# Two matmul groups and one split of the next expert, moved into both arms of a data-dependent branch

## Chip, cores and metric

The kernel runs on one NeuronCore of a Trainium2 chip. The metric is the device time of one execution in microseconds (us), as the median of several runs.

## What is computed

One layer of a hybrid decoder on 2048 tokens of width 1024: a normalisation and a combined projection, a gated MLP branch and a gated linear recurrence, their merge, then a mixture of experts (MoE), and last a gated per-layer embedding and a final normalisation. The change touches the mixture of experts alone:

```python
def expert_block(args):                     # for each block of tokens of expert e
    xb, e = args
    return (jax.nn.silu(xb @ w1[e]) * (xb @ w3[e])) @ w2[e]
...
grp_prob = jax.nn.softmax(grp_logits, axis=-1)      # top-1 group of 4
top_l, top_e = lax.top_k(sel_logits, TOP_K)         # top-2 of the 8 experts in it
```

There are 32 experts (N_EXPERTS), with w1 and w3 of 1024 x 512 and w2 of 512 x 1024 each, and 4096 assignments of tokens to experts. How many tokens an expert gets depends on the data: 128 on the average, more for some and fewer for others.

## The kernel before

All products are in float32 precision. The large ones are made of float32r matmuls with each operand split into a high and a low part (hi and lo): ScalarE (ACT) copies the raw chunk into float32r, VectorE (DVE) subtracts the copy from the raw chunk, and TensorE (PE) adds three products, hi x hi, lo x hi and hi x lo.

The experts run one after the other in a loop of 33 turns (lines 1071 to 1110), under a manual schedule: each engine takes its instructions in the order in which the program emits them. Turn i has three experts in hand: `was` (the one before), `now` and `then` (the next). An expert takes its first 128 tokens through the split products. Its w1 and w3 come as eight chunks of 128 rows, its w2 as four. The order within a turn is written out by hand in the string `PART`, a word for each step:

- `h2`, `l2` are the high and low split of chunk 2 (methods `hi`, line 890, on ACT; `lo`, line 896, on DVE), and `H0 L0 H1 L1` those of the next expert's chunks 0 and 1. `v0 u0 v1 u1` split chunks of w2. The split tiles `ehi` and `elo` have five buffers each (`SPL`).
- `P0` to `P7` are the matmul groups of the chunks, six matmuls of 512 columns each (line 905), added up in two PSUM banks `ph` of the pool `ps_a`, which has four.
- `S` is the silu on ACT (line 910) and the product with the other half on DVE (line 911), into the tile `g`. `T` is four PE transposes of `g` (line 916), `G` the split of the result, `B0` to `B3` the matmuls with w2 (line 937), `Y` the copy out and the scattered write. These are steps of `was`, a turn after its P7.
- `X`, `x`, `y` turn and split the next expert's token rows.
- `n` and `m` write branch hints, for POOL and SP and for PE, ACT and DVE.

At the end of the turn stands a branch on the count of `now`, read from a register: with more than 128 tokens all engines run `some(0)` (line 945), for 32 more tokens; inside it stand two more branches, for more than 160 tokens `some(1)`, and for more than 192 `rest`. `some` is a chain: 64 small matmuls `pa` (line 950), a silu on ACT (line 954), a product on DVE (line 955), one transpose on PE (line 956), a copy on DVE (line 958), 32 small matmuls `pz` (line 961), a copy on ACT (line 965) and a scattered write.

```python
with tc.If((code & bit) != 0, preferred_fallthrough_block=True, label=f"more{i}"):
    skip(f"most{i}", code, 2 * bit, BUSY[:1])
    now.some(0)
    with tc.If((code & 2 * bit) != 0, preferred_fallthrough_block=True, label=f"most{i}"):
        ...
```

`skip` writes the hint for a later branch: here that of the inner branch `most`, for PE, ahead of `some(0)`. An engine that passes an arm by must still bring its semaphores to the count that the arm would have brought them to; it does so by event instructions, which stand in the profile on the line of the branch (L1103 for the outer branch, L1106 for `most`, L1109 for `beyond`). A program that skips `some` altogether goes from P7 of `now` over the branch to the first words of the next turn, `S P0 P1 h2 l2 h3 l3 T G P2`, in which S and T belong to the expert just finished and P0, P1, h2 and P2 to the next one.

The weights of the next expert are loaded by SP at the head of a turn (lines 720 and 727), into buffers that the expert before last has read to the end, its branch included.

Of the kernel before, what the change touches and what calls it, by code (L numbers as in the profile page):

```python
# [9 lines left out]
F32R = mybir.dt.float32r  # L10
# [7 lines left out]
BUSY = [mybir.EngineType.PE, mybir.EngineType.Activation, mybir.EngineType.DVE]  # L18
QUEUED = [mybir.EngineType.Pool, mybir.EngineType.SP]
# [5 lines left out]
T = 2048  # L25
D = 1024
KT = D // 128
# [9 lines left out]
EPG = 8  # L37
# [7 lines left out]
SPL = 5  # L45
W2B = 8
HGRN = "forget0 R query0 R decay0 og0 R og20 forget1 R att0 query1 state0 decay1 og1 read0 R og21 forget2 R R R norm0 att1 query2 decay2 og2 state1 forget3 read1 R norm1 att2 og22 og3 query3 R state2 decay3 R G og23 att3 G read2 G state3 norm2 G read3 norm3"
PART = "n S P0 P1 h2 l2 h3 l3 T G P2 B0 X h4 l4 B1 h5 l5 x B2 h6 l6 y B3 h7 l7 P3 P4 Y v0 u0 m P5 v1 u1 P6 H0 L0 P7 H1 L1"
ORDER = [EPG * g + i for i in range(EPG) for g in (0, 1, 3, 2)]
EARLY = 4  # L50
E0 = 0, 0, 2, 2
# [25 lines left out]
def tile_hybrid_block(ctx: ExitStack, tc: tile.TileContext, a, out):  # L77
# [3 lines left out]
    x = a["x"][0]  # L81
# [16 lines left out]
    def mm():  # L98
        return ps_a.tile([128, 512], F32, name="pa")

    def px():
        return ps_b.tile([128, 512], F32, name="pb")
# [45 lines left out]
    with ExitStack() as fin, ExitStack() as route_ctx, ExitStack() as moe_ctx:  # L148
# [16 lines left out]
        def u(name, dt=F32):  # L165
            return wk.tile([128, TB], dt, name=name, tag="u")
# [20 lines left out]
        def split(src):  # L187
            hi = u("hi", F32R)
            act.activation(hi, src, AF.Copy)
            lo = u("lo", F32R)  # L190
            vec.tensor_tensor(lo, src, hi.bitcast(F32), op=OP.subtract)
            return hi, lo
# [327 lines left out]
        def gated(w_up, gate0, j, h_t, y):  # L520
            ps = fm(w_in, gate0 + 128 * j, h_t)
            s = u("sgate")
            act.activation(s, ps, AF.Sigmoid)
            ps = fm(w_up, 128 * j, y)
            vec.tensor_tensor(s, ps, s, op=OP.mult)
            return s
# [210 lines left out]
        for b in range(NB):  # L737
# [41 lines left out]
            for j in range(8):  # L779
                s = gated(a["w_up_b"][0], 4096, j, h_t, yb)  # L780
# [24 lines left out]
        code = sm.tile([1, 3, NG], F32, name="code")  # L805
        for j, top in enumerate((128.0, 160.0, 192.0)):
            bit = C["bits"][:, j]
# [5 lines left out]
        xe = moe_ctx.enter_context(tc.tile_pool(name="xe", bufs=1, side="right", reuse_waits="tile"))  # L813
# [42 lines left out]
        class Expert:  # L856


            def __init__(self, i):
                self.e = ORDER[i]  # L860
                self.parts = {}
                self.py = []

            def fetch(self):
# [20 lines left out]
            def raw(self, k):  # L885
                return self.w13[k] if k < KT else self.w2[k - KT].rearrange("p (n c) -> p n c", n=2)

            def hi(self, k):
                t = xe.tile([128, 2, 512], F32R, name="ehi", tag="ehi", bufs=SPL)
                act.activation(t, self.raw(k), AF.Copy)  # L890
                self.parts[k] = t, None

            def lo(self, k):
                hi = self.parts[k][0]
                t = xe.tile([128, 2, 512], F32R, name="elo", tag="elo", bufs=SPL)
                vec.tensor_tensor(t, self.raw(k), hi.bitcast(F32), op=OP.subtract)  # L896
                self.parts[k] = hi, t

            def P(self, k):
                if k == 0:  # L900
                    self.ph = [mm() for _ in range(2)]
                hi, lo = self.parts.pop(k)
                for w, xp in ((hi, self.xhi), (lo, self.xhi), (hi, self.xlo)):
                    for n in range(2):
                        pe.matmul(self.ph[n], xp[:, k], w[:, n], start=k == 0 and w is hi and xp is self.xhi,  # L905
                                  stop=k == KT - 1 and xp is self.xlo)
# [35 lines left out]
                    act.activation(y[:, 512 * c:512 * c + 512], self.py[c], AF.Copy)  # L942
                put(y, yi[:, self.e:self.e + 1])

            def some(self, s):

                pa, pt, pz = px(), px(), px()
                for k in range(KT):
                    for q in range(4):
                        pe.matmul(pa[32 * q:32 * q + 32, 0:256], self.xr[:, k, 128 + 32 * s:160 + 32 * s],  # L950
                                  self.w13[k][:, :, 128 * q:128 * q + 128], start=k == 0, stop=k == KT - 1,
                                  skip_group_check=True)
                t = xl.tile([128, 128], F32, name="sg", tag="sg", bufs=2)
                act.activation(t, pa[:, 0:128], AF.Silu)
                vec.tensor_tensor(t, pa[:, 128:256], t, op=OP.mult)
                pe.transpose(pt[:, 0:128], t, ident)
                st = xl.tile([128, 128], F32, name="st", tag="sg", bufs=2)
                vec.tensor_copy(st, pt[:, 0:128])
                for k in range(4):
                    for q in range(4):  # L960
                        pe.matmul(pz[32 * q:32 * q + 32, 0:256], st[:, 32 * k:32 * k + 32],
                                  self.w2[k][:, 256 * q:256 * q + 256], start=k == 0, stop=k == 3,
                                  skip_group_check=True)
                yz = xl.tile([128, 256], F32, name="yz", tag="yz", bufs=1)
                act.activation(yz, pz[:, 0:256], AF.Copy)
                put(yz, ym[s][:, self.e:self.e + 1])
# [57 lines left out]
        ex = [Expert(i) for i in range(NE)]  # L1024
# [24 lines left out]
        codes_r, loads = [], []  # L1049

        def skip(label, code, bit, engines):
            tc.mark_branch_hint_location(label, (code & bit) // bit, engines=engines)

        def load(src, top):
            done = len(nc.cur_bb.bb.instructions)
            n = nc.values_load(src, min_val=0, max_val=top)
            loads.extend(nc.cur_bb.bb.instructions[done:])
            return n
# [8 lines left out]
        in_order(done)  # L1067
        for g in range(NG):
            codes_r.append(load(codes[0:1, g:g + 1], 8 ** EPG - 1))
        with tc.manual_schedule():  # L1070
            for i in range(NE + 1):
                was, now, then = (ex[j] if 0 <= j < NE else None for j in (i - 1, i, i + 1))
                if then:
                    then.w13, then.w2 = list(load_expert(i + 1))[-1]
                    if i == 0:
                        first.clear()
                elif now:
                    nc.sync.dma_start(gple, a["g_ple"][0].rearrange("(n p) -> p n", p=128))
                    for k2 in range(PGE):
                        load_pg(k2)  # L1080
                    praw = xe.tile([128, MB, PLE], F32, name="praw0", tag="rows", bufs=2)
                    ple_rows(0, praw)
                if i + 2 < NE:
                    ex[i + 2].fetch()
                if now is None:
                    ple_turn(praw, pT)
                for word in PART.split():
                    name, k = word[0], int(word[1:] or 0)
                    if name in "STGBY":
                        if was:  # L1090
                            getattr(was, name)(*([k] if name == "B" else []))
                    elif name in "HLXxy":
                        if then:
                            getattr(then, {"H": "hi", "L": "lo"}.get(name, name))(*([k] if name in "HL" else []))
                    elif now and name in "nm":
                        code, bit = codes_r[now.e // EPG], 8 ** (now.e % EPG)
                        skip(f"more{i}", code, bit, {"n": QUEUED, "m": BUSY}[name])
                    elif now:
                        if name in "vu":
                            k += KT  # L1100
                        getattr(now, {"h": "hi", "l": "lo", "v": "hi", "u": "lo"}.get(name, name))(k)
                if now:
                    with tc.If((code & bit) != 0, preferred_fallthrough_block=True, label=f"more{i}"):  # L1103
                        skip(f"most{i}", code, 2 * bit, BUSY[:1])
                        now.some(0)
                        with tc.If((code & 2 * bit) != 0, preferred_fallthrough_block=True, label=f"most{i}"):  # L1106
                            skip(f"beyond{i}", code, 4 * bit, BUSY[:1])
                            now.some(1)
                            with tc.If((code & 4 * bit) != 0, preferred_fallthrough_block=True, label=f"beyond{i}"):  # L1109
                                now.rest()  # L1110

        moe_ctx.close()
        wg_p = fin.enter_context(tc.tile_pool(name="wg_p", bufs=1, side="right", reuse_waits="tile"))
# [162 lines left out]
        begun = len(nc.cur_bb.bb.instructions)  # L1276
# [33 lines left out]
```

## Time and profile before

| | |
|---|---|
| median of three runs | 2488.26 us (2485.77 to 2488.78) |
| the profiled execution's own time | 2473.56 us |
| its span, first to last instruction | 2471.8 us |
| the loop over the experts | about 1487 to 2241 us of the span |
| granted TensorE clock, mean | 0.992 of full speed |

The span is what the rows below divide up; 1.8 us lie around it. PE is TensorE's matmuls, DVE is VectorE, ACT is ScalarE, and SP issues the loads. A letter q behind an engine (PEq, ACTq) is its sequencer, which branches, waits and counts; PEldq is that of PE. A row of the time-ordered view that says x2 merges two instructions, and the arrow behind it says for how long the engine had been idle and what ended that.

### The profile page before, as it was taken

Reading aid. Unit: us, or ns where it says so; the run is one execution under the profiler, and the core shown is the slowest. Engines: PE = TensorE matmul, PEld = TensorE weight load, DVE = VectorE, ACT = ScalarE, POOL = GpSimd, SP = SyncE. Lnnn points to the kernel's source line nnn. Section 1 sums busy time; section 2 is a strip of 40 time slices with the busy share of each in tenths; the row PEclk is TensorE's granted clock in tenths of the full one; section 3 lists DMA queues with packets and bytes.
Section 4 is the critical chain, followed back from the end, with each engine's and each line's share of the span. In section 5 each row is a group of like instructions: output and inputs, shape, how many; then the busy total and the mean of one; then the engine's idle time right before and its main releaser. Section 6 shows DMA issues by size and latency. Waiting matters only on the chain. (4 is left out here: it accounts for less than half of the span.)

```text
span 2471.8 us, 38160 instructions
## 1 busy us (share of the span) xinstructions
PE 2362.5 (96%) x13676; PEld 1901.6 (77%) x13676; DVE 1449.1 (59%) x2505; ACT 1281.4 (52%) x1964; POOL 393.2 (16%) x371
## 2 busy tenths in 40 slices
PE   7999999999999999999999989999889989898998
PEld 6898898888898988998978946666666666665887
DVE  6564445763545753446644346667566767675776
ACT  6763345753446643447633246556555656565443
POOL 1000000100000100000200043344334434331000
PEclk9999999999999999999999999999999999999999
DMA  5333443234342234432343478788778878795553
GB/s 171 95 90 91 130 151 89 76 105 132 116 135 75 82 108 132 132 116 69 106 125 94 141 253 303 269 330 310 278 284 326 322 279 331 281 341 205 200 218 126
DMA packets 313093, 445.81 MB, mean 180 GB/s; under 512 B 32442, under 2 KB 231174, under 8 KB 310752
## 3 DMA queue, kind: packets, MB, share of 16 engines
q1 hardware_dynamic: 290272, 385.68, 46.0%
q0 software_dynamic: 22528, 56.46, 6.3%
q8 instruction: 155, 2.54, 0.4%
q14 instruction: 138, 1.13, 0.1%
HBM read 401.87 MB, written 51.02 MB: 183 GB/s over the span
## 5 line engine op out<-in xcount | busy, mean ns | idle before, releaser
L180 DVE TENSOR_TENSOR wlo<-wraw,whi 128x512 fp32r<-128x512 f32 x445 | 305.4, 688 | 423.0 <-ACT whi L179 395.2
L179 ACT ACTIVATE whi<-wraw 128x512 fp32r<-128x512 f32 x448 | 281.3, 628 | 519.8 <-PE pa L204 326.0
L203 PE MATMUL pa<-h,whi 128*128 128x512 f32 x1024 | 403.7, 394 | 0.0
L204 PE MATMUL pa<-h,whi 128*128 128x512 f32 x1024 | 399.9, 391 | 0.0
L205 PE MATMUL pa<-h,wlo 128*128 128x512 f32 x1024 | 399.6, 390 | 0.0
L896 DVE TENSOR_TENSOR elo<-w13r,ehi 128x1024 fp32r<-128x1024 f32 x256 | 308.2, 1218 | 53.3 <-ACT ehi L890 38.5
L890 ACT ACTIVATE ehi<-w13r 128x1024 fp32r<-128x1024 f32 x256 | 263.3, 1054 | 56.4 <-PE pa L905 53.1
L839 POOL DMA_INDIRECT rows<-h_d,tokidx x192 | 240.0, 1250 | 286.2 <-issue 100.4
L203 PEld LDWEIGHTS pa<-h,whi 128*128 128x128 f32 x1024 | 192.4, 188 | 41.9 <-issue 0.7
L205 PEld LDWEIGHTS pa<-h,wlo 128*128 128x128 f32 x1024 | 192.3, 188 | 40.9
L204 PEld LDWEIGHTS pa<-h,whi 128*128 128x128 f32 x1024 | 192.5, 188 | 39.4
L905 PE MATMUL pa<-ehi,xhi 128*128 128x512 f32 x512 | 185.9, 440 | 36.0 <-ACTq L1106 10.8
L905 PE MATMUL pa<-ehi,xlo 128*128 128x512 f32 x512 | 164.8, 403 | 6.8 <-DVE xlo L883 6.8
L905 PE MATMUL pa<-elo,xhi 128*128 128x512 f32 x512 | 164.8, 403 | 6.8 <-issue 6.5
L905 PEld LDWEIGHTS pa<-ehi,xhi 128*128 128x128 f32 x512 | 94.9, 193 | 84.7 <-ACTq L1106 15.1
L223 PE MATMUL pa<-whi,h 128*128 128x256 f32 x512 | 146.2, 286 | 0.1
L224 PE MATMUL pa<-wlo,h 128*128 128x256 f32 x512 | 145.3, 284 | 0.0
L225 PE MATMUL pa<-whi,h 128*128 128x256 f32 x512 | 145.2, 284 | 0.0
L223 PE MATMUL pa<-whi,hi 128*128 128x256 f32 x512 | 143.6, 281 | 0.0
L224 PE MATMUL pa<-wlo,hi 128*128 128x256 f32 x512 | 143.5, 280 | 0.0
L225 PE MATMUL pa<-whi,lo 128*128 128x256 f32 x512 | 143.2, 280 | 0.0
L905 PEld LDWEIGHTS pa<-ehi,xlo 128*128 128x128 f32 x512 | 98.9, 193 | 34.0 <-DVE xlo L883 7.2
(320 smaller groups left out, 4524.6 us busy)
## 6 DMA issues: line engine op xcount, KB each, us to landing
w13r<-in_w_dram SPq DMA_DIRECT2D x256, 512.0 KB, 8.0
wraw<-in_w_in_dram SPq DMA_DIRECT2D x320, 256.0 KB, 2.9
w2r<-in_w_dram SPq DMA_DIRECT2D x128, 512.0 KB, 11.4
wraw<-in_w_out_dram SPq DMA_DIRECT2D x64, 256.0 KB, 2.8
yt<-y_d SPq DMA_DIRECT2D x16, 1024.0 KB, 5.8
xt<-in_x_dram SPq DMA_DIRECT2D x32, 256.0 KB, 3.8
wraw<-in_w_up_a_dram SPq DMA_DIRECT2D x32, 256.0 KB, 3.0
wraw<-in_w_up_b_dram SPq DMA_DIRECT2D x32, 256.0 KB, 2.9
```

The lines of the kernel that those rows point to most:

```text
L179: whi = act.activation(hi, raw, AF.Copy)
L180: wlo = (pool if n < POOLG else vec).tensor_tensor(lo, raw, hi.bitcast(F32), op=OP.subtract)
L203: pe.matmul(ps, hi[:, k4], xhi, start=k == 0, stop=False)
L204: pe.matmul(ps, hi[:, k4], xlo, start=False, stop=False)
L205: pe.matmul(ps, lo[:, k4], xhi, start=False, stop=k == n_k - 1)
L223: pe.matmul(o, xhi[:, s], hi[:, k2], start=st, stop=False, skip_group_check=True)
L224: pe.matmul(o, xhi[:, s], lo[:, k2], start=False, stop=False, skip_group_check=True)
L225: pe.matmul(o, xlo[:, s], hi[:, k2], start=False, stop=k == n_k - 1, skip_group_check=True)
L839: ins = pool.indirect_dma_start(out=g[:, q], out_offset=None, in_=h2_d, in_offset=bass.IndirectOffsetOnAxis(ap=idx[:, at:at + 1], axis=0), ...
L890: act.activation(t, self.raw(k), AF.Copy)
L896: vec.tensor_tensor(t, self.raw(k), hi.bitcast(F32), op=OP.subtract)
L905: pe.matmul(self.ph[n], xp[:, k], w[:, n], start=k == 0 and w is hi and xp is self.xhi, stop=k == KT - 1 and xp is self.xlo)
```

## The change

P0, h2, l2 and P1 of the next expert no longer stand at the head of the next turn. They now stand in both arms of the outer branch. In the arm that is taken, h2, P0 and l2 come between the product and the transpose of `some(0)`, and P1 between the copy of the transpose and `pz`; the second `some` has nothing put into it. The other arm is new and holds `P0 h2 l2 P1`. S of the expert just finished stands at the end of its own turn, ahead of the branch. T, h3, G and l3 follow the branch at once. The two PSUM banks of the next expert and the split tiles of its chunk 2 are now allotted ahead of the branch, so that both arms write the same ones. The hint for `most` is written just ahead of `pz`, behind P1, and no longer ahead of `some(0)`. Expert 0 has P0, h2, l2, P1 ahead of the loop.

```diff
-PART = "n S P0 P1 h2 l2 h3 l3 T G P2 B0 X h4 l4 ... H0 L0 P7 H1 L1"
+BEGIN = "P0 h2 l2 P1"
+GAPS = "h2 P0 l2", "P1"
+PART = "n h3 T G l3 P2 B0 X h4 l4 ... H0 L0 P7 H1 L1 S"
...
+            def keep(self, ks):
+                self.ph = [mm() for _ in range(2)]
+                self.kept = {(name, k): self.split(name, k) for k in ks for name in ("ehi", "elo")}
...
-            def some(self, s):
+            def some(self, s, gaps):
...
                 vec.tensor_tensor(t, pa[:, 128:256], t, op=OP.mult)
+                next(gaps, None)
                 pe.transpose(pt[:, 0:128], t, ident)
                 st = xl.tile([128, 128], F32, name="st", tag="sg", bufs=2)
                 vec.tensor_copy(st, pt[:, 0:128])
+                next(gaps, None)
...
+        def gaps(x, words, label, code, bit):
+            for i, some in enumerate(words):
+                if x:
+                    do(x, some)
+                if i == len(words) - 1:
+                    skip(label, code, bit, BUSY[:1])
+                yield
...
+                if then:
+                    then.keep((2,))
+                    begun = dict(then.parts)
                 if now:
-                    with tc.If((code & bit) != 0, preferred_fallthrough_block=True, label=f"more{i}"):
-                        skip(f"most{i}", code, 2 * bit, BUSY[:1])
-                        now.some(0)
+                    with tc.If((code & bit) != 0, preferred_fallthrough_block=True, label=f"more{i}") as more:
+                        now.some(0, gaps(then, GAPS, f"most{i}", code, 2 * bit))
...
+                    if then:
+                        then.parts = begun
+                        with more.Else():
+                            do(then, BEGIN)
```

## Rows read from the trace of the kernel before

**Rows 1.** Stretches: us, engines' busy time, clock, DMA share, GB/s.
```profile
1487.50:2241.00 753.50, 690.53 (x4102) 480.29 (x4100) 500.99 (x474) 436.42 (x538) 273.70 (x224) 0.99 0.81 303
1891.16:1916.89 25.73, 23.97 (x170) 16.35 (x170) 16.30 (x16) 14.19 (x18) 10.29 (x8) 1.00 0.77 288
...
2065.95:2084.87 18.92, 18.32 (x73) 13.14 (x73) 15.73 (x15) 13.56 (x17) 9.28 (x7) 1.00 1.03 399
```

**Rows 2.** Waits of PE in 1487 to 2241: total us, times, longest.
```profile
PE pb L956 <- DVE sg L955: 13.7, 19, 0.7
PE pa L905 <- ACTq L1106: 10.8, 9, 3.5
PE pa L905 <- ACT ehi L890: 7.6, 3, 2.6
PE pa L905 <- issue: 6.5, 2, 3.4
PE pb L961 <- issue: 6.5, 15, 0.4
PE pa L905 <- DVEq L1103: 4.2, 14, 0.3
PE pa L905 <- PEq L1103: 4.2, 14, 0.3
PE pa L905 <- ACTq L1103: 3.1, 1, 3.1
PE pa L905 <- ACTq L1109: 2.3, 3, 0.8
PE pa L905 <- PEq L1106: 2.1, 1, 2.1
```

**Rows 3.** PE in order of time, over a branch that is passed by.
```profile
1519.71 0.64 PE L905 MATMUL pa<-ehi,xlo 128*128 128x512 f32 x2
1520.64 0.47 PE L905 MATMUL pa<-ehi,xhi 128*128 128x512 f32 x1 [0.30 <-PEq L1103]
1521.41 0.50 PE L905 MATMUL pa<-ehi,xhi 128*128 128x512 f32 x1 [0.30 <-DVEq L1103]
1521.74 0.62 PE L905 MATMUL pa<-elo,xhi 128*128 128x512 f32 x2
...
1524.07 0.60 PE L916 MATMUL pb<-ident,g 128*128 128x128 f32 x4
```

**Rows 4.** ACT in order of time, same place.
```profile
1520.24 0.60 ACT L910 ACTIVATE g<-pa 128x512 f32<-128x512 f32 x1 [0.20 <-ACTq L1103]
1520.73 1.05 ACT L890 ACTIVATE ehi<-w13r 128x1024 fp32r<-128x1024 f32 x1
1522.87 1.06 ACT L890 ACTIVATE ehi<-w13r 128x1024 fp32r<-128x1024 f32 x1 [1.09 <-PE pa L905]
```

**Rows 5.** DVE in order of time, same place.
```profile
1521.65 0.69 DVE L911 TENSOR_TENSOR g<-pa,g 128x512 f32<-128x512 f32 x1 [0.35 <-DVEq L1103]
1522.26 1.21 DVE L896 TENSOR_TENSOR elo<-w13r,ehi 128x1024 fp32r<-128x1024 f32 x1
```

**Rows 6.** PE in order of time, through an arm that is taken.
```profile
1539.18 3.66 PE L950 MATMUL pb<-w13r,xr 128*32 128x256 f32 x64
1543.56 0.33 PE L956 MATMUL pb<-ident,sg 128*128 128x128 f32 x1 [0.72 <-DVE sg L955]
1544.32 1.94 PE L961 MATMUL pb<-w2r,st 128*32 128x256 f32 x32 [0.43 <-issue]
1548.78 0.73 PE L905 MATMUL pa<-ehi,xhi 128*128 128x512 f32 x2 [2.52 <-ACT ehi L890]
```

**Rows 7.** ACT in order of time, same arm.
```profile
1542.91 0.28 ACT L954 ACTIVATE sg<-pb 128x128 f32<-128x128 f32 x1 [3.96 <-PE pb L950]
```

**Rows 8.** PE's sequencer, branches of L1103 and L1106: count, ns min/median/max.
```profile
L1103 PEldq COMPARE_BRANCH  x32: 75/227/3347, 1489.5 to 2237.0; - x32
...
L1106 PEldq COMPARE_BRANCH  x29: 71/200/3440, 1499.2 to 2222.9; - x29
```

More of the change, by code (lines that the diff above doesn't have):

```diff
@@ L47 @@
 HGRN = "forget0 R query0 R decay0 og0 R og20 forget1 R att0 query1 state0 decay1 og1 read0 R og21 forget2 R R R norm0 att1 query2 decay2 og2 state1 forget3 read1 R norm1 att2 og22 og3 query3 R state2 decay3 R G og23 att3 G read2 G state3 norm2 G read3 norm3"
-PART = "n S P0 P1 h2 l2 h3 l3 T G P2 B0 X h4 l4 B1 h5 l5 x B2 h6 l6 y B3 h7 l7 P3 P4 Y v0 u0 m P5 v1 u1 P6 H0 L0 P7 H1 L1"
+BEGIN = "P0 h2 l2 P1"
+GAPS = "h2 P0 l2", "P1"
+PART = "n h3 T G l3 P2 B0 X h4 l4 B1 h5 l5 x B2 h6 l6 y B3 h7 l7 P3 P4 Y v0 u0 m P5 v1 u1 P6 H0 L0 P7 H1 L1 S"
 ORDER = [EPG * g + i for i in range(EPG) for g in (0, 1, 3, 2)]
@@ L861, in __init__ @@
                 self.parts = {}
+                self.kept = {}
                 self.py = []
@@ L886, in raw, with split @@
                 return self.w13[k] if k < KT else self.w2[k - KT].rearrange("p (n c) -> p n c", n=2)
+            def split(self, name, k):
+                return self.kept.get((name, k)) or xe.tile([128, 2, 512], F32R, name=name, tag=name, bufs=SPL)
+            def keep(self, ks):
+                self.ph = [mm() for _ in range(2)]
+                self.kept = {(name, k): self.split(name, k) for k in ks for name in ("ehi", "elo")}
             def hi(self, k):
-                t = xe.tile([128, 2, 512], F32R, name="ehi", tag="ehi", bufs=SPL)
+                t = self.split("ehi", k)
                 act.activation(t, self.raw(k), AF.Copy)
@@ L894, in lo @@
                 hi = self.parts[k][0]
-                t = xe.tile([128, 2, 512], F32R, name="elo", tag="elo", bufs=SPL)
+                t = self.split("elo", k)
                 vec.tensor_tensor(t, self.raw(k), hi.bitcast(F32), op=OP.subtract)
@@ L899, in P @@
             def P(self, k):
-                if k == 0:
-                    self.ph = [mm() for _ in range(2)]
                 hi, lo = self.parts.pop(k)
@@ L1069, in tile_hybrid_block, with do @@
             codes_r.append(load(codes[0:1, g:g + 1], 8 ** EPG - 1))
+        def do(x, words):
+            for word in words.split():
+                name, k = word[0], int(word[1:] or 0)
+                if name in "vu":
+                    k += KT
+                name = {"h": "hi", "v": "hi", "H": "hi", "l": "lo", "u": "lo", "L": "lo"}.get(name, name)
+                getattr(x, name)(*([k] if word[1:] else []))
+        def gaps(x, words, label, code, bit):
[5 more added lines that the diff above has]
+                yield
         with tc.manual_schedule():
+            ex[0].keep(())
+            do(ex[0], BEGIN)
             for i in range(NE + 1):
@@ L1087, in tile_hybrid_block @@
                 for word in PART.split():
[L1088 to L1101, printed above, removed]
+                    if word in "nm":
+                        if now:
+                            code, bit = codes_r[now.e // EPG], 8 ** (now.e % EPG)
+                            skip(f"more{i}", code, bit, {"n": QUEUED, "m": BUSY}[word])
+                        continue
@@ L1102, in tile_hybrid_block @@
+                    x0 = was if word[0] in "TGBY" else then if word[0] in "HLXxy" else now
+                    if x0:
+                        do(x0, word)
+                if then:
+                    then.keep((2,))
+                    begun = dict(then.parts)
                 if now:
-                    with tc.If((code & bit) != 0, preferred_fallthrough_block=True, label=f"more{i}"):
-                        skip(f"most{i}", code, 2 * bit, BUSY[:1])
-                        now.some(0)
+                    with tc.If((code & bit) != 0, preferred_fallthrough_block=True, label=f"more{i}") as more:
+                        now.some(0, gaps(then, GAPS, f"most{i}", code, 2 * bit))
@@ L1106, in tile_hybrid_block @@
                         with tc.If((code & 2 * bit) != 0, preferred_fallthrough_block=True, label=f"most{i}"):
-                            skip(f"beyond{i}", code, 4 * bit, BUSY[:1])
-                            now.some(1)
+                            now.some(1, gaps(None, GAPS, f"beyond{i}", code, 4 * bit))
                             with tc.If((code & 4 * bit) != 0, preferred_fallthrough_block=True, label=f"beyond{i}"):
                                 now.rest()
+                    if then:
+                        then.parts = begun
+                        with more.Else():
+                            do(then, BEGIN)
```

## The prediction

> **What bounds the kernel now.** I read the stretches first, to see whether the expert loop is a PE stage. It is: PE is busy for 690.5 of its 753.5 us [rows 1], and no other engine is near that. So what PE loses in the loop is all there is to win, at most 63 us, some 2.5% of the kernel. Two kinds of turn show in the same view: one that passes the branch by takes 18.92 us with 18.32 us of PE, and one that takes the outer arm 25.73 us with 23.97 us. The DMA share is 1.03 in the short turn and 0.77 in the long one, so loads fill the short turns completely and have room in the long ones. Next the waits of PE [rows 2]: they sort the loss by place, and their counts give the kinds of turns. The transpose L956 waits 19 times, once for each run of `some`; the waits on L1109 say that 3 of these are second runs. So 16 turns take the arm, 13 of them skip the inner one, and 15 turns that have a next expert pass by (14 with waits for DVEq and PEq of L1103, one with a long wait for ACTq). Then PE in order of time over a passed branch [rows 3] and through a taken arm [rows 6], with ACT and DVE beside them [rows 4, 5, 7], to see what each wait is for. Last the branches themselves [rows 8].
>
> **The passed branch.** In [rows 3] the last pair of P7 starts at 1519.71 and T at 1524.07, 4.36 us for seven pairs. A pair takes 0.466 us when nothing holds it (five pairs in the 2.33 us from 1521.74 to T), so seven take 3.26 us and 1.10 us is lost. It goes in two places. First PE drains: the event on L1103 that stands for the skipped arm waits until P7 is done, which costs 0.30 us of idle time and the overlap of one matmul with the next (0.40 us for a last one, 0.23 us from start to start), 0.47 us in all. The rest is the second matmul of P0, which waits for DVE to come past the branch: that bank's last reader in program order is in the skipped arm. With the change P0 and P1 stand in the other arm and write banks allotted a turn ahead, whose readers are long past, so I take the second wait as gone. The drain stays, since the events must still be made up; it moves behind P1, ahead of T. Gain 1.10 - 0.47 = 0.63 us, 15 times: 9.4 us. Bounds: if T or P2 waits for DVE's event, 0.25 us less in each turn (below); if no drain is left, all 1.10 us.
>
> What is late next? S on ACT already starts at P7's end [rows 4] and goes on doing so. On DVE the split that precedes the product ends at 1521.30 (the product's start less its idle 0.35, [rows 5]); the product now follows it without a branch between, ends near 1522.0, and l2 behind the branch ends near 1523.6 (1.21 us of work). P2 wants l2 at its third matmul: 2.80 us for P0 and P1, 0.47 drain, 0.35 for T (its 0.60 us [rows 3] less the overlap) and 0.47 for its first pair after 1520.18, which is 1524.27. It fits by 0.6 us. h3 on ACT waits for P0's buffer [rows 4]; in the new arm PE may tell that only at its event behind P1, so h3 starts some 1.1 us later against T, and G behind it. G's first part then ends about 1.4 us after T starts, and B0 begins at 1.75. That fits too, by 0.35 us. The loads at the head of a turn wait for the same event of PE and so start 2.8 us later against P7, but as much of the next turn's PE work is then already done, so against P2 they are where they were. The hint words and S's place cost nothing by themselves: S lies under the first matmuls behind the branch.
>
> **The taken arm.** In [rows 6] `pa` starts its last matmul some 0.33 us before 1542.84, so another could start at 1542.5; `pz` starts at 1544.32, 1.82 us later. All of it is the chain silu, product, transpose, copy. Put between: P0 and P1, 2.80 us of matmuls that the next turn then doesn't have. ACT's silu ends at 1543.19 [rows 7], h2 behind it takes 1.05 us [rows 4], and l2 1.21 us [rows 5]; since the copy that `pz` waits for stands behind l2 on DVE, it comes at about 1543.2 + 1.05 + 0.2 + 1.21 + 0.3 = 1545.95. PE reaches `pz` at 1545.3 at the earliest, so the loss is about 0.65 us in place of 1.82. Gain 1.17 us, 16 times: 18.7 us. Bounds: 0.8 us each if B0 then waits 0.35 us for G; 1.7 us if l2 is out of the way.
>
> Behind `pz` a quiet turn loses 25.73 - 23.97 - 0.72 - 0.43 = 0.61 us [rows 1, 6], the inner branch's drain and jump. I leave it as it is. In all 16 turns these waits are 10.8 + 7.6 + 2.3 + 2.1 = 22.8 us [rows 2], 13.0 us more than 16 x 0.61. That surplus is late code: the branch of L1106 takes 3.4 us at worst and 0.2 us at the median [rows 8]. I leave it too, and the 6.5 us that PE waits twice with no releaser [rows 2], since where a jump lands badly will be dealt anew. One wait does go: the 3.1 us in which a passed branch waited for ACT [rows 2]. P0 and P1 don't need ACT there, and they last 2.8 us: 2.5 us gained.
>
> **The sum.** 9.4 + 18.7 + 2.5 = 30.6 us. The profiled execution took 2473.56 us, so 2443.0 us of its own time. The median of the runs lies 14.7 us above that execution, with the same program; I take the same gain there: 2488.26 - 30.6 = 2457.7 us. A change under 0.2%, 5 us, can't be told from none here.
>
> **Rivals.**
>
> *The late hint.* The hint for `most` stood before `pa`, over 5 us ahead of `pz`; now it stands just ahead of it. If it no longer has time to work, each of the 13 skips pays what [rows 6] shows for a bad one, 2.52 - 0.61 = 1.91 us: 24.8 us, of which 13.0 us at most are in the time already. The gain falls by 11.8 us: 2469.5 us. For it: a full wait for code is 3.4 us [rows 8], more than `pz` lasts (1.94 us). Against it: bad skips occur with the early hint as well, and `pz` still covers part. The opposite, a late hint that cures the bad ones, is the low end of the range: up to 9 us more.
>
> *The loads bind.* In the short turns the DMA share is 1.03 at 399 GB/s [rows 1]; if they can't be shortened, the 9.4 us go: 2467 us. Against it: short turns mostly alternate with long ones at 0.77, and PE's waits name no DMA [rows 2].
>
> *The splits set the pace.* DVE works 15.73 of 18.92 us in a short turn [rows 1], each split waiting for a buffer that PE frees. If order on DVE and ACT eats what PE wins, the time stays within 0.2% of 2488 us. Against it: 3.2 us are free for the 0.63 us that I take.
>
> *Slower: code behind the jump.* The new arm adds 12 matmuls with their weight loads to the far side of every passed branch, and the taken arm must jump over them. Today a passed branch takes up to 3.35 us in PE's sequencer [rows 8] and is hidden, because P5 to P7 are still queued; a wait for code right behind it isn't: the two waits on "issue" cost 3.25 us each [rows 2]. If each of 15 passed turns met one such wait, 49 us would go: 2506 us. It decides from the tenth on (30.6 / 3.25). For it: no passed branch resolves without a wait of some length. Against it: behind the jump come as many instructions as before, and only two of 31 turns show such a wait.
> The Trainium skill, "Runtime: NRT & Kernel Launch", Instruction fetch mechanics, says that a taken branch whose target is not among the pages at hand forces a fetch before the engine can go on, and it would put that charge on every passed branch and every skip. The trace agrees only in part: the median skip or jump on L1106 takes 0.2 us and only some take over 3. By the rule alone the sum would be that of this rival together with the late hint, 2506 + 12 = 2518 us; by the rows it is the 2457.7 above.
>
> **How the numbers follow.** Forecast 0.57 (gains of 22 to 40 us, 2448 to 2466 us), late hint 0.13, loads 0.11, within 0.2% 0.09, slower 0.10. The first three are faster: 0.81. The range leaves out the last two and takes in the bounds: up to 2477 us (late hint, 2469.5, with most of the 9.6 us that the low bounds take off, 5.7 + 12.8 in place of 28.1), down to 2441 us (forecast, and part of the late code or the upper bounds besides). The likeliest time is 2458 us.
>
> **What would show it.** In the profile after, the waits for L955 and L958 ahead of `pa`'s transpose and `pz` should be nearly gone for 16 of 19 runs and stay for the 3 second ones, with a wait of about 0.5 us of `pz` for the copy. PE should start P0 0.23 us after P7's last matmul where the branch is passed, with one drain of 0.3 us ahead of T and none for DVE. A short turn should last about 18.3 us and a quiet long one 24.5 us. It is wrong if P2, T or B0 shows a wait in most turns, if waits of 2 to 3.5 us behind L1103 or L1106 grow in number, or if S or h3 come later and hold B0.

## The result, and the profile after

The change made the kernel 1.1% faster: 2457.7 us against 2487.0 us, ratio 0.989 (95% interval 0.987 to 0.991). The forecast was 2458 us. That the total agrees to a microsecond is in part luck: the gain in the turns without long waits was larger than worked out, and a wait that was counted as gained did not go. The experiments were needed to see it.

The stretches of after, columns as in [rows 1] (the engines are PE's matmuls, PE's weight loads, DVE, ACT and POOL): the expert loop from the start of the first P2 to that of the last, a quiet passed turn and a quiet taken one.

```profile
1488.19:2211.55 723.36, 679.74 (x4056) 467.40 (x4055) 485.98 (x468) 425.16 (x528) 288.12 (x224) 0.98 0.83 311
1517.36:1535.40 18.04, 17.99 (x74) 13.12 (x73) 15.61 (x15) 13.56 (x16) 6.92 (x7) 1.00 1.03 401
2019.84:2044.34 24.50, 23.77 (x171) 16.02 (x170) 15.93 (x16) 13.84 (x18) 7.02 (x6) 1.00 0.76 279
```

Against [rows 1] the passed turn went from 18.92 to 18.04 us and the taken one from 25.73 to 24.50. PE is now busy for all but 0.05 us of the passed turn, at the same DMA share of 1.03. The waits of PE in that stretch, columns as in [rows 2]; L914 is now the matmuls of P, L925 T, L966 the transpose in `some`, L972 `pz`, L959 `pa`:

```profile
PE pb L925 <- ACTq L1131: 14.4, 11, 3.4
PE pb L966 <- DVE sg L964: 4.4, 4, 2.3
PE pb L925 <- PEq L1131: 4.2, 2, 2.2
PE pb L925 <- ACTq L1133: 3.9, 2, 3.2
PE pb L925 <- DVE elo L907: 3.7, 2, 3.4
PE pa L914 <- ACT ehi L901: 3.6, 2, 2.4
PE pa L914 <- issue: 2.5, 2, 2.2
PE pb L959 <- issue: 2.3, 4, 0.8
...
PE pb L972 <- DVE st L968: 0.8, 2, 0.4
```

The waits for the product ahead of the transpose fell from 13.7 us in 19 to 4.4 us in 4: three are the second runs of `some`, which got no filling, and one is a late one. The 0.30 us waits for DVEq and PEq of L1103, 14 of each, are gone. Behind a taken arm T is now first and has the wait that P0 had (L1131). What didn't go are waits of 2 us and more, scattered over several lines. PE over a passed branch, P7's last pair, P0, P1 and T in one run:

```profile
1520.96 0.62 PE L914 MATMUL pa<-ehi,xlo 128*128 128x512 f32 x2
1521.43 0.62 PE L914 MATMUL pa<-ehi,xhi 128*128 128x512 f32 x2
...
1523.74 0.63 PE L914 MATMUL pa<-ehi,xlo 128*128 128x512 f32 x2
1524.43 0.63 PE L925 MATMUL pb<-ident,g 128*128 128x128 f32 x4
```

From P7's last pair to T it is 3.47 us now and was 4.36 in [rows 3]; seven pairs take 3.26. PE in a taken arm, and DVE beside it:

```profile
1496.95 3.66 PE L959 MATMUL pb<-w13r,xr 128*32 128x256 f32 x64
1500.54 0.72 PE L914 MATMUL pa<-ehi,xhi 128*128 128x512 f32 x2
...
1502.04 0.27 PE L966 MATMUL pb<-ident,sg 128*128 128x128 f32 x1
1502.07 0.71 PE L914 MATMUL pa<-ehi,xhi 128*128 128x512 f32 x2
...
1503.08 0.64 PE L914 MATMUL pa<-ehi,xlo 128*128 128x512 f32 x2
1503.64 1.93 PE L972 MATMUL pb<-w2r,st 128*32 128x256 f32 x32
1506.38 0.63 PE L925 MATMUL pb<-ident,g 128*128 128x128 f32 x4 [0.80 <-ACTq L1131]
```

```profile
1500.99 0.29 DVE L964 TENSOR_TENSOR sg<-pb,sg 128x128 f32<-128x128 f32 x1 [1.62 <-ACT sg L963]
1501.94 1.23 DVE L907 TENSOR_TENSOR elo<-w13r,ehi 128x1024 fp32r<-128x1024 f32 x1 [0.65 <-ACT ehi L901]
1503.08 0.28 DVE L968 COPY st<-pb 128x128 f32<-128x128 f32 x1
```

From the start of `pa` to that of `pz` it is 6.69 us with P0 and P1 inside, and was 5.14 us without them [rows 6]. The copy ends at 1503.36, before PE is through P1's last pair (1503.08 + 0.64): in this turn the chain of `some` has left the path. The branches in PE's sequencer, columns as in [rows 8], L1129 the outer and L1131 the inner one:

```profile
L1129 PEldq COMPARE_BRANCH  x32: 75/394/6487, 1493.2 to 2222.2; - x32
L1131 PEldq COMPARE_BRANCH  x29: 71/200/2929, 1504.1 to 2210.8; - x29
```

The longest wait on the outer branch is 6.5 us here and was 3.3 us in [rows 8]; the kernel before shows 6.4 us as well when it is profiled again (below).

### The profile page after: what moved, and what is told of

It reads as the page before. It is cut to its first block, busy times and chain, and to the rows that moved or that the text cites. A ratio compares the mean times of both kernels' runs of the same rounds, so it can differ in the third digit from the quotient of the medians.

```text
span 2457.3 us, 38163 instructions
## 1 busy us (share of the span) xinstructions
PE 2364.7 (96%) x13676; PEld 1898.8 (77%) x13676; DVE 1440.3 (59%) x2505; ACT 1277.6 (52%) x1963; POOL 410.2 (17%) x371
## 5 line engine op out<-in xcount | busy, mean ns | idle before, releaser
L841 POOL DMA_INDIRECT rows<-h_d,tokidx x192 | 256.2, 1334 | 301.3 <-DVE elo L907 107.0
L914 PE MATMUL pa<-ehi,xhi 128*128 128x512 f32 x512 | 182.2, 437 | 7.9 <-ACT ehi L901 3.6
L914 PE MATMUL pa<-ehi,xlo 128*128 128x512 f32 x512 | 164.2, 402 | 8.2 <-DVE xlo L886 8.2
L914 PE MATMUL pa<-elo,xhi 128*128 128x512 f32 x512 | 164.0, 402 | 0.9 <-DVE elo L907 0.8
L914 PEld LDWEIGHTS pa<-ehi,xhi 128*128 128x128 f32 x512 | 93.2, 193 | 47.5 <-issue 29.3
L914 PEld LDWEIGHTS pa<-ehi,xlo 128*128 128x128 f32 x512 | 98.3, 192 | 31.9 <-DVE xlo L886 8.6
```

Source lines behind the costliest of these rows:

```text
L841: ins = pool.indirect_dma_start(out=g[:, q], out_offset=None, in_=h2_d, in_offset=bass.IndirectOffsetOnAxis(ap=idx[:, at:at + 1], axis=0), ...
```

## The experiments

For each run the text calls a turn the time from the first matmul of P2 to that of the next expert's P2, sorts the turns into 15 passed, 13 taken and 3 that also take the inner arm, and calls quiet the shortest of its kind. Late code is then the sum of turns 1 to 30 less as many quiet ones; in the profiles these surpluses are waits of PE behind branches, and the slow matmuls after them, at a lower clock. That PE or another engine waits there for its instructions is a reading; no row shows a fetch. Turn 0 is left out of it, being shorter. Where a kind has no quiet turn (passed without hints; both arms in the kernel with longer code), that of after is taken. All are worked out from the starts of P2 in each trace. Ratios are to the kernel before on the same chip.

| kernel | ratio (95% interval) | passed, us | taken, us | late code, us |
|---|---|---|---|---|
| before, first profile | | 18.91 | 25.70 | 31 |
| before, again | 0.999 (0.998 to 1.000) | 18.91 | 25.70 | 41 |
| after | 0.989 (0.987 to 0.991) | 18.05 | 24.51 | 46 |
| filling ahead of `some` | 0.999 (0.997 to 1.000) | 18.05 | 25.73 | 48 |
| early inner hint | 0.989 (0.987 to 0.992) | 18.05 | 24.5 | 47 |
| after without rest | 0.976 (0.975 to 0.978) | 18.09 | 24.4 | 10 |
| before without rest | 0.983 (0.982 to 0.985) | 18.24 | 25.6 | 6 |
| after, longer code | 0.989 (0.986 to 0.992) | 18.05 | 24.5 | 34 |
| after, no hints | 1.002 (1.000 to 1.003) | 20.1 | 24.5 | 71 |
| after, filler for rest | 0.983 (0.982 to 0.985) | 18.1 | 24.4 | 32 |
| rest behind the loop, 4 branches | 0.984 (0.982 to 0.986) | 18.05 | 24.4 | 11 |
| rest behind the loop, 1 branch | 0.976 (0.974 to 0.977) | 18.05 | 24.3 | 11 |
| the same with a hint | 0.976 (0.974 to 0.977) | 18.05 | 24.3 | 12 |

**Before, once more.** No edit.

> The kernel before, unchanged, as a second execution to read. In the first pair of profiles the loop of experts got 18.5 us shorter (747.5 to 729.0 us from its first branch to its last), while the medians of the runs differ by 29 us. Theory A: the quiet turns (no late code) are the same in every execution, 18.9 us passed and 25.7 us taken, and what differs from execution to execution is late code, which was lucky in the first profile of before; then this profile shows 18.9 and 25.7 again, and its loop is 747 us plus whatever its waits of 2 to 3.5 us add. Theory B (rival): the whole stage runs slower in most executions, for example because loads hold it, and then the quiet turns themselves are longer here. Timed against itself the ratio is 1.00.

The quiet turns are the same to 0.02 us. The loop from the first P2 to the last is 750.6 us here and was 742.1 in the first profile; late code is 41 us and was 31. Theory A holds. All timed runs of the kernel before lie between 2475 and 2494 us, and the first profile, with 2473.6 us, was a lucky execution. Of the 12.9 us between the two profiled executions (2486.4 us for the second) the loop makes 8.6; the rest lies elsewhere.

```profile
L1103 PEldq COMPARE_BRANCH  x32: 75/227/6412, 1492.1 to 2248.4; - x32
L1106 PEldq COMPARE_BRANCH  x29: 71/200/3896, 1501.1 to 2234.2; - x29
```

Against [rows 8] the same 32 branches took up to 6.4 us where they had taken 3.3: the same program, another draw.

**The taken arm alone undone.**

```diff
 with tc.If((code & bit) != 0, ...) as more:
-    now.some(0, gaps(then, GAPS, f"most{i}", code, 2 * bit))
+    if then:
+        do(then, BEGIN)
+    now.some(0, gaps(None, GAPS, f"most{i}", code, 2 * bit))
```

> As after, but in the taken arm P0, h2, l2 and P1 stand ahead of some(0) in place of inside it; the other arm is unchanged. Theory A (two separate gains, one for each arm): the taken arm's gain goes and the passed one stays, so quiet taken turns go from 24.5 back to 25.7 us with waits of 0.7 and 0.4 us for L964 and L968 in 16 turns, passed turns stay at 18.0 us, and the time is 16 x 1.2 = 19 us above after, about 2477 us, 0.4 to 0.5% under before. Rival: the gain of both comes from S and the banks standing ahead of the branch, and the filling is worth little: within 5 us of after.

2479.0 us, 21 us above after by the medians and 24 by the ratios; the loops differ by 23 us, of which 16 turns longer by 1.2 us are most and late code 2. The waits are back, as they were in [rows 2]:

```profile
PE pb L966 <- DVE sg L964: 16.0, 19, 1.4
...
PE pb L972 <- DVE st L968: 3.8, 10, 0.4
```

So the filling is worth what it looks to be worth, and it is not S or the banks that do it. The other half is the surprise: passed turns are 0.86 us shorter than before, 12.9 us in all, and yet the kernel is within 0.3% of before. Its late code is 48 us against 41 and its turn 0 is 1.6 us longer, so its loop is only 4.3 us shorter than that of before's second profile (746.4 and 750.6).

**The inner hint back at its old place.**

```diff
 with tc.If((code & bit) != 0, ...) as more:
+    skip(f"most{i}", code, 2 * bit, BUSY[:1])
     now.some(0, gaps(then, GAPS, f"most{i}", code, 2 * bit))     # gaps writes no hint for most
```

> As after, but the hint for the inner branch is written ahead of some(0), where before had it. Theory (late hint is as good or better): the branch on the inner arm takes 3.0 to 3.4 us again in some 5 of 13 skips, in place of 1.1 to 2.9 us, hidden in part under pz, and the time is 0 to 6 us above after. Rival (the late hint costs): skips get shorter and the time is 5 to 12 us under after.

The same time as after, 2456.2 us. Of 13 skips 2 take 2 us or more, with the late hint 3, in before 5. Where this hint stands makes no measurable difference. The theory's small loss wasn't seen either.

**Without the innermost arm.**

```diff
-with tc.If((code & 4 * bit) != 0, ..., label=f"beyond{i}"):
-    now.rest()
```

> As after, without the innermost arm (rest, for experts of more than 192 tokens), which no expert of this input enters. It leaves out the handling of such experts; the code that every jump passes over is then shorter by the arm and its loop. Theory (late code is what the loop still loses, some 46 us over its quiet turns in the profile of after, and it hangs on how far the jumps go and where they land): quiet turns stay at 18.0 and 24.5 us, the waits of 2 us and more get fewer, and the time falls by 10 to 30 us under after. Rival (late code hangs on the loads that fill the DMA queues, not on the distance): within 5 us of after.

2423.3 us, 34 us below after by the medians, nearly all of it late code: 46 us became 10, while the quiet turns stayed within 0.15 us (those with two runs of `some` are 0.5 us shorter). Of PE's 10 waits of 2 us or more in the loop, 25.5 us in all, three with 8.0 us are left, and the mean granted clock of the loop is 1.00 in place of 0.98. The code that goes has never run. Its waits and branches:

```profile
PE pb L925 <- ACTq L1131: 10.3, 13, 2.8
PE pb L925 <- DVE elo L907: 2.8, 1, 2.8
PE pb L925 <- ACT ehi L901: 2.4, 1, 2.4
PE pb L966 <- DVE sg L964: 2.2, 3, 0.7
```

```profile
L1129 PEldq COMPARE_BRANCH  x32: 66/496/2106, 1489.5 to 2180.2; - x32
L1131 PEldq COMPARE_BRANCH  x32: 71/198/1718, 1500.7 to 2168.8; - x32
```

The median of the outer branch is no shorter than in after. What is gone is the upper end, 6.5 and 2.9 us there, 2.1 and 1.7 us here; a wait of 2 us is covered by P5 to P7 in the queue, one of 6 isn't: here the passed turns with branches of 1.9 to 2.1 us last 18.1 to 18.4 us, in after those with 6.25 and 6.49 us last 21.8 and 20.5.

**Before without the innermost arm.** The same edit, and the hint for it, in the kernel before.

> The kernel before without the innermost arm (rest), which no expert of this input enters; it leaves out the handling of experts with more than 192 tokens. Two things are told apart. First the passed branch: by the prediction, P0's second matmul waits for DVE because its PSUM bank was last read in rest. If that is so, the wait for DVE goes with rest and the drain of 0.3 us stays: passed turns go from 18.9 to 18.3 us, taken ones stay at 25.7. If the wait has another cause, passed turns stay at 18.9 us. Second late code: if it hangs on the distance of the jumps, the waits of 2 us and more get fewer here too, by 20 to 35 us in all, and the time is 2440 to 2455 us; if it is special to after, about 2475 us.

2437.2 us. Passed turns are 18.24 us, as the prediction's account of P0's second matmul asks: with no `rest` to read the bank last, the wait for DVE goes and the drain stays. PE over a passed branch:

```profile
1565.40 0.62 PE L905 MATMUL pa<-ehi,xlo 128*128 128x512 f32 x2
1566.17 0.70 PE L905 MATMUL pa<-ehi,xhi 128*128 128x512 f32 x2
...
1569.05 0.60 PE L916 MATMUL pb<-ident,g 128*128 128x128 f32 x4
```

Both matmuls of P0's first pair now go together; P7's last pair to T is 3.65 us, 0.39 over seven pairs. So of the 0.86 us that the change takes off a passed turn, 0.67 is the bank's reader and 0.19 the drain. Late code is 6 us here, so it isn't a thing of the new arm alone. Between the two kernels without rest the change is worth 0.976 / 0.983, 0.7% or about 17 us.

**More code to pass over.**

```diff
 with tc.If((code & 4 * bit) != 0, ..., label=f"beyond{i}"):
+    now.some(1, iter(()))
     now.rest()
```

> As after, with a further copy of some(1) inside the innermost arm, which no expert of this input enters; every jump over that arm passes some 195 more PE instructions, and nothing more is done. Theory (late code hangs on the distance of the jumps): quiet turns stay at 18.0 and 24.5 us, the waits of 2 us and more grow, and the time is 10 to 40 us above after. Rival (what counts is where the jumps happen to land, not how far they go): within 10 us of after, on either side.

The same ratio as after, and 34 us of late code against 46: the theory in this form falls. With this much more code, farther is not worse.

**As much code, of another kind.**

```diff
 with tc.If((code & 4 * bit) != 0, ..., label=f"beyond{i}"):
-    now.rest()
+    now.some(1, iter(()))
```

> As after, with the innermost arm's rest replaced by a further copy of some(1): about as much PE code to pass over (some 200 instructions in place of 145), but no loop, no loads and little code for the other engines. It leaves out the handling of experts with more than 192 tokens, of which this input has none. Theory (late code comes of the length of PE's code that a jump passes, over some bound that the kernels without rest stay under): as after, about 2455 us, within 10 us, with waits of 2 to 3.5 us in some ten turns. Rival (it comes of what rest is: its loop, its loads and its code on ACT, DVE and POOL): as without rest, 2423 to 2430 us.

2441.8 us, 0.6% under after and 0.7% above the kernel without rest; late code 32 us. Neither side is right: other code in the same place brings most of it back (10 to 32 us), and the rest of the 46 us, 14 us of device time by the ratios, comes of something in which the two kernels differ: what `rest` is, or where the jumps land.

**No hints for PE, ACT and DVE.**

```diff
-            skip(f"more{i}", code, bit, {"n": QUEUED, "m": BUSY}[word])
+            if word == "n":
+                skip(f"more{i}", code, bit, QUEUED)     # and none for most and beyond
```

> As after, without any branch hint for PE, ACT and DVE in the loop (those for POOL and SP stay). Theory (the outer hint gets the far side under way while P5 to P7 are still queued): passed branches take about 3.4 us or more in PE's sequencer in place of 0.7 to 2, some of them show behind P7, and the time is 10 to 40 us above after. Rival (the hints are without effect, as the place of the inner one was): within 5 us of after.

2483.0 us, 25 us above after by the medians and 1.3%, 31 us, by the ratios. The outer hint matters:

```profile
L1130 PEldq COMPARE_BRANCH  x32: 78/1750/7726, 1490.7 to 2247.0; - x32
```

Of the 16 passed branches 14 take 6.06 to 6.30 us, one 3.4 and one 7.7. With the hint 12 of 16 take 0.7 to 1.9 us and the other four 4.2 to 6.5, two of them as long as without a hint. Quiet taken turns are as in after, with as much late code in turns of one run (20 us against 21). Six of the 13 skips take 2 us or more, against three in after and five in before, so no use of the inner hint shows in the time.

**Rest behind the loop.** Two versions for any counts. The weights of an expert with more than 192 tokens are loaded a second time; no expert of this input is one.

```diff
-with tc.If((code & 4 * bit) != 0, ..., label=f"beyond{i}"):
-    now.rest()
...                                            # behind the loop, first version: for each of four groups
+with tc.If((codes_r[g] & over) != 0, ...):
+    for j in range(EPG):
+        with tc.If((codes_r[g] & 4 * 8 ** j) != 0, ...):
+            x0.w13, x0.w2 = list(load_expert(...))[-1]
+            x0.rest()
...                                            # second version: once, for all groups
+every = codes_r[0] | codes_r[1] | codes_r[2] | codes_r[3]
+with tc.If((every & over) != 0, ...):
+    for e in range(NE): ...                    # as above, for each expert
```

> A version that computes the whole layer for any counts: as after, but the innermost arm (rest) no longer stands in each turn. Behind the loop stand four branches, one for each group, that are taken if an expert of the group has more than 192 tokens; in them the weights of such an expert are loaded again and rest runs. Theory (late code hangs on how much code the jumps of a turn pass over): the loop is as without rest, and four jumps over a lot of code cost up to 3.5 us each at its end; the time is 2425 to 2440 us, 2 to 2.4% under before. Rival (the end of the loop is on the path of the last stage and these jumps hold its loads): above 2445 us.

> The version that computes the whole layer for any counts, with one branch behind the loop in place of four: it is taken if any expert has more than 192 tokens, and branches for each expert stand inside it. In the version with four, ACT came past them 15 us after the first. Theory (each far jump is one wait for code of about 3.7 us on ACT and PE, whatever its length): 11 us under the version with four, about 2427 us, 2.1% under before. Rival (the longer jump costs more, or SP's loads are held all the same): 2432 us or more.

> As the version with one branch behind the loop, with a hint for PE, ACT and DVE at the head of the last turn that says that it is passed by. Theory (a hint well ahead gets the far side fetched): up to 4 us under the version without it. Rival (such a hint comes too early, as the inner branch's had no effect, or the place behind the loop isn't on the path): the same within 2 us.

With four branches 2438.4 us: the loop is as short as without rest, but ACT stands still between them:

```profile
2197.96 0.60 ACT L951 ACTIVATE y<-pb 128x512 f32<-128x512 f32 x1 [0.26 <-PE pb L946]
2216.48 2.19 ACT L1296 ACTIVATE pghi<-pgraw,gple 128x1024 fp32r<-128x1024 f32 x2 [17.93 <-issue]
```

With one branch 2420.9 us, 2.4% under before, and the hint adds nothing. That is 17 us under the version with four by the medians and 21 by the ratios, where three jumps at 3.7 us made 11. The profiles show 13 us of it on ACT, which stands idle at this place for 17.93 us with four branches and 5.05 us with one. On this input, where no arm behind the loop runs, this version beats both kernels.

## Why the forecast came out right

**The passed branch.** The mechanism was right: a drain, and a bank whose last reader stands in the skipped arm. The kernel before without rest shows the second part by itself. The size was low: 0.86 us each in place of 0.63, 12.9 us in place of 9.4. The term that was mis-sized is "The drain stays ... it moves behind P1", at 0.47 us. T still starts only when P1's last matmul has ended (1524.43 against 1523.74 + 0.63), but 0.06 us behind it and not 0.30, and the drain costs 0.2 us. So the gain lies between the 0.63 and the upper bound of 1.10, for which no drain would be left.

**The taken arm.** 1.19 us each in place of 1.17, and 1.36 in the turns with two runs; with turn 0 some 19.6 us against 18.7. The copy that `pz` waits for came 6.4 us after `pa`'s start, where I had worked out 6.8, and PE got to `pz` at 6.7, so the half microsecond of waiting that I expected is not there. That the size fits is luck: the copy came 0.4 us sooner and PE 0.6 us later than worked out, since P0 began 3.59 us after `pa` and not 3.32, and the transpose between the pairs (0.27 us) was left out of PE's path. The run with the filling ahead of `some` gives the gain as 21 to 24 us of device time.

**Late code.** Here a term of the sum failed. I left late code alone but for one wait of 2.5 us that I took as gained, since P0 and P1 don't need ACT (how 2.5 comes out of the 3.1 and 2.8 us beside it the prediction doesn't say). That step was wrong: T behind them waits for l2 on DVE, so an engine that comes late past the branch still holds PE. In the turn that begins at 2052.11, the longest passed one with 24.70 us, PE's own branch took 1.76 us; DVE began l2 2.95 us after the product with no releaser in the trace, and T came 3.4 us after P1's end:

```profile
2074.69 1.23 DVE L907 TENSOR_TENSOR elo<-w13r,ehi 128x1024 fp32r<-128x1024 f32 x1 [2.95 <-issue]
2076.07 1.09 PE L925 MATMUL pb<-ident,g 128*128 128x128 f32 x4 [3.41 <-DVE elo L907]
```

PE's waits of 2 us or more in the loop did not grow: 9 with 25.7 us and 10 with 29.2 in before's two profiles, 10 with 25.5 in after. The late code of the table is 31 and 41 us for before and 46 for after; two profiles of one program are 10 us apart, so the 5 us between 41 and 46 are not shown to come of the change. Passed turns have 21 us of it in after, and 6 and 9 in before, but 8 of the 21 are five turns that begin at the lower clock, just behind a long wait of T that the count puts into the turn before.

Quiet turns gained 32.5 us (15 x 0.86, 12 x 1.19, 3 x 1.36 and 1.2 for turn 0). The loops of before's second profile and of after differ by 27.3 us (750.6 and 723.4), so between these two late code took back 5.2. The ratio gives 27.6 us, with an interval from 22 to 34 that doesn't tell the two apart. My 30.6 us were 28.1 + 2.5: too little by 4.4 in the quiet turns and, for this pair of profiles, too much by 7.7 in late code. Taking the gain off the median and not off the profile was luckier than I knew: against that lucky first profile, after's is only 14.5 us shorter.

**The rivals.** The late hint did nothing, as the run with the early one shows; three bad skips in place of five. The loads didn't bind: a passed turn runs in 18.04 us at 401 GB/s, so the share of 1.03 in the longer turn before wasn't a limit. The splits didn't set the pace, as PE is busy for 17.99 of these 18.04 us. The slower rival, code behind the jump, was the one that had something in it: between two profiles it took back 5 us, no more than one program's own spread, and in the run with the taken arm undone it took most of the 12.9 us of the passed arm. It stayed far from the ten long waits at which it would have decided. The Trainium skill's rule ("Runtime: NRT & Kernel Launch", Instruction fetch mechanics), that a taken branch to a page not at hand stalls for a fetch, agrees with these runs in what it is about: without the hint a passed branch takes 6.1 us in PE's sequencer nearly every time, and without `rest`, with the hint, none takes over 2.1. As a charge on the time of every jump it does not agree: with the hint 12 of 16 passed branches take 0.7 to 1.9 us, which the matmuls in the queue cover.

**What stays open.** Late code hangs on the innermost arm (6 to 12 us without it in the turns, 30 and more with it), but it didn't grow in the one kernel with a longer arm (34 us), and a filler that is mostly PE code brings back 32 of 46 us. Whether the rest comes of the other engines' code, which holds PE in the turn at 2052.11, or of where the 31 jumps happen to land wasn't tried, and that any of it is the fetching of code was argued and not shown.

## What to carry to other kernels

Work that both arms of a branch need can fill the waits of the arm that is taken, and it starts without the joint waits behind the branch if its buffers are allotted ahead; look who read a buffer last in program order, even in an arm that never runs. Code that never runs isn't free: here a rare arm in each turn of an unrolled loop cost 1.3% without being entered, so try it behind the loop, under one branch. And take more than one profile where branches are many, since a single one may be ten microseconds from the next.

## What was not expected of the hardware

A far jump without a hint took 6.1 us in PE's sequencer, with remarkable regularity (14 of 16 within 0.25 us); with a hint some 36 instructions ahead it took 0.7 to 1.9 us in 12 of 16, and moving the same kind of hint for the inner branch left the time as it was (0.989 at either place).

A long wait can cost more than its length. In after, T came 3.4 us late at 2076.07, and the stretches of 2 us around it show the granted clock, the third column from the right:

```profile
2074.00:2076.00 2.00, 0.00 (x0) 0.00 (x0) 1.23 (x1) 0.00 (x0) 1.70 (x2) 0.99 1.01 385
2076.00:2078.00 2.00, 1.94 (x7) 1.77 (x8) 0.39 (x2) 0.38 (x1) 0.82 (x1) 0.50 1.04 394
2078.00:2080.00 2.00, 2.00 (x8) 1.59 (x7) 1.16 (x2) 1.62 (x3) 0.00 (x0) 0.66 1.00 310
2080.00:2082.00 2.00, 2.00 (x10) 1.61 (x9) 1.86 (x2) 0.82 (x2) 0.00 (x0) 1.00 1.00 403
```

After the wait it is 0.50, the lower of the two levels (1.2 GHz), and then 0.66 on the average of a stretch, with pairs of matmuls 0.8 to 1.0 us apart in place of 0.47. Of the 10 waits of 2 us or more in after's loop six were followed by the lower level and four were not; behind the waits of 0.7 to 0.8 us the granted clock is 1.00 each time. So some of the late code in the table is a lower clock.
